# A hybrid S5 and attention trunk: the S5 stage with its first input columns in halves, chunks in pairs, two blocks in float32, and its stages in another order

## The chip, the cores and the metric

The kernel runs on one core of one Trainium2 chip. The metric is the time of one execution on the device, in microseconds (us). A core has five engines that run on their own, each in the order of its own queue: TensorE (PE, matrix products, with weight loads listed as PEld), VectorE (DVE), ScalarE (ACT), GpSimd (POOL), and SyncE (SP), which here only issues DMAs. They wait for each other at semaphores.

## The reference

Two layers on 256 tokens of width 1024, all in float32. Each layer adds half a SwiGLU of the normed stream, then a mixer, then half another SwiGLU. The first layer's mixer is an S5 state-space layer, the second's a block-sparse attention. The change concerns S5:

```python
u = h @ w_in                                     # 256 x 1024, 64 groups of 16 columns
bu = einsum(u, bb)                               # per group: 16 inputs -> 64 complex states
st = associative_scan(lam, bu)                   # st[t] = lam * st[t-1] + bu[t], complex
y = real part of einsum(st, c) + d_skip * u
g = gelu(y)
g = g * sigmoid(g @ w_glu)
h = h + g @ w_out
```

## The kernel before, in words

One program does the phases f00, s5, f01, f10, moba and f11 one after the other. `f..` are the feed-forward parts. Weights come from memory as raw float32 units of 1 MB in three buffers (class `Stream`, `RAW = 3`). A unit is loaded into a buffer as soon as the unit three places before it is freed. Each unit has two halves. `split` turns a half into a high part (`whi`, ACT, L84 or L90) and a low part (`wlo`, DVE, L85 or L91) in a format that TensorE multiplies in one pass; when the second half is split, the raw buffer is free. A product of two float32 matrices is then three products, high by high, high by low, low by high (`mm3`). `st.pump()` splits the next half ahead of its use, where the code calls it: the splits take their place in the queues of ACT and DVE at that point. The order of instructions in each queue is the order of the Python calls; nothing moves them.

S5 works through 8 blocks of 128 columns. The steps, with the lines of the profile:

- `w_in(nh, t)` (L397 to L399, tile pM): half of the columns (512) for token half t, 24 products; ACT copies the result to `us` (L976), DVE transposes it in 32x32 pieces into `U` (L977). Four calls.
- `t1(b)` (L986): block b of U times a table TA, 16 small float32 products; the result is in pA for the first four blocks and in one of the two pM buffers after that.
- `rot(b)`: on DVE two products with a table TE (L1006, L1007), a difference and a sum into `zi` (L1008, L1009), and two scans along time into `zo` (L1011); then on POOL two products (L1015, L1016) and a sum and a difference (L1017, L1018) into `hr`. The filling `rh` of the scan comes from ACT (L995), and two memsets (L994, L1005) from DVE.
- `y_out(b)` (L1044): 24 small float32 products of U and hr with a table TB into one of the two PSUM buffers pR; ACT applies Gelu into `yg`, of which there is one (L1048); DVE transposes it into `gs`, of which there are two (L1051).
- `g_tr(b)` (L1060): TensorE transposes gs into a pR buffer; ACT makes the high part of g (L1062), DVE the low part (L1063), ACT then a float32 copy `gf` (L1064).
- `glu(b)` (L1077 to L1079): block b of `g @ w_glu`, transposed, 8 column blocks of 3 products of 256 columns, accumulated over b in pA 0 to 3. `gate(i)` (L1088 to L1093): sigmoid, product with gf, high and low part.
- `so(b, t, n)` (L397 to L399, tile pA): the product with w_out.

The order around the change, `t1` and `rot` running some blocks ahead of `y_out` and `glu`:

```python
        w_in(1, 0, {3: [lambda: t1rot(0)], 5: [lambda: t1rot(1)]})
        w_in(1, 1, {1: [lambda: t1rot(2)], 4: [lambda: t1ld(3)]}, ())
        ...
        for b in range(3, NB):
            y_out(b)
            glu(b - 3)
            if b + 3 < NB:
                t1rot(b + 3)
            g_tr(b - 1)
```

A hook `{3: [...]}` is called before the fourth of the eight row blocks of a product. The tables TA, TE and TB (three buffers each) are loaded by SP (`ld_a`, `ld_e`, `ld_b`), in one queue with the weights.

Of the kernel before, what the change touches and what calls it, by code (L numbers as in the profile page):

```python
# [118 lines left out]
def trunk_kernel(ctx: ExitStack, tc, x, ffn_norm, ffn_w_gate, ffn_w_up, ffn_w_down, mix_norm,  # L119
# [3 lines left out]
    nc = tc.nc  # L123
# [28 lines left out]

    units = []
    where = {}
    GAIN = {"f00": None, "f01": 8, "f10": 16, "f11": 24, "s5": 32, "moba": 40}

    def add(key, load, gains=None):

        where[key] = len(units)
        units.append((key, load, gains))  # L160

    ahead = []

# [34 lines left out]
    def s5_units():  # L198
        for nh in range(2):
            for a in range(2):  # L200
                add(("win", nh, a), ld_cols(s5_w_in[0], a * 512, nh * 512), GAIN["s5"] + 4 * a)
        for b in range(4):
            add(("glu", b), ld_rows(s5_w_glu[0], b * 256))
        for b in range(4):
            add(("so", b), ld_rows(s5_w_out[0], b * 256))

    QKV = [("k", 0), ("q", 0), ("k", 1), ("q", 1), ("v", 0), ("v", 1)]
    QOFF = {"q": 0, "k": 1024, "v": 2048}
# [749 lines left out]
    def s5(nxt, entry):  # L958
# [12 lines left out]
        def w_in(nh, t, hooks, pumps=(1, 5)):  # L971
            uA, uB = where["win", nh, 0], where["win", nh, 1]
# [3 lines left out]
            nc.scalar.activation(us, ps, AF.Identity, scale=Rr[t])  # L976
            V.transpose(U[:, nh * 16:(nh + 1) * 16, t, :], us.rearrange("p (q c) -> p q c", c=32))  # L977

        def t1(b):
            tv = TA.pop(b).rearrange("p (i q c) -> p i q c", i=2, c=128)  # L980
# [5 lines left out]
                        mm(ps[r, c:c + 64], tv[:, i, q, r], U[:, 4 * b + q, :, :], start=True, stop=True)  # L986
            S[b] = ps

        def rot(b):
            sv = S.pop(b).rearrange("p (i q c) -> p i q c", i=2, c=64)  # L990
            e = TE.pop(b)
            ec, es = (e[:, None, i] for i in range(2))
            rh = wp.tile([128, 4, 65], F32, name="rh", bufs=2)
            V.memset(rh[:, :, 0:1], 0.0)  # L994
# [3 lines left out]
            zi = wp.tile([128, 2, 4, 65], F32, name="zi", bufs=1)  # L998
# [7 lines left out]
            V.tensor_tensor(wv[0], sv, bc(ec, 1), op=OP.mult)  # L1006
            V.tensor_tensor(wv[1], sv, bc(es, 1), op=OP.mult)  # L1007
            V.tensor_tensor(zi[:, 0, :, 1:65], wv[0][:, 0], wv[1][:, 1], op=OP.subtract)  # L1008
            V.tensor_tensor(zi[:, 1, :, 1:65], wv[0][:, 1], wv[1][:, 0], op=OP.add)  # L1009
            for i in range(2):  # L1010
                V.tensor_tensor_scan(zo[:, i].rearrange("p q c -> p (q c)"),  # L1011
                                     rh.rearrange("p q c -> p (q c)"),
                                     zi[:, i].rearrange("p q c -> p (q c)"), 0.0, op0=OP.mult, op1=OP.add)
            z = zo[:, :, :, 0:64]
            P.tensor_tensor(pv[0], z, bc(ec, 0), op=OP.mult)  # L1015
# [5 lines left out]
        def t1ld(b):  # L1021
            t1(b)
            if b + 3 < NB:
                ld_a(b + 3)

        def t1rot(b):
            t1ld(b)
            rot_ld(b)

        def rot_ld(b):  # L1030
            rot(b)
            if 0 < b < NB - 2:
                ld_e(b + 2)

        def y_out(b):
            tb = TB.pop(b)
            v2 = tb[:, 0:1024].rearrange("p (i q c) -> p i q c", i=2, c=128)
            v3 = tb[:, 1024:1536].rearrange("p (q c) -> p q c", c=128)
            ps = psR()
            hr = H.pop(b)  # L1040
            for q in range(4):
                for i, (v, z) in enumerate(((v3[:, q], U[:, 4 * b + q]), (v2[:, 0, q], hr[:, 0, q]), (v2[:, 1, q], hr[:, 1, q]))):
                    for r in HALVES:
                        mm(ps[r, q * 64:(q + 1) * 64], v[:, r], z, start=i == 0, stop=i == 2)  # L1044
# [3 lines left out]
            nc.scalar.activation(yg.rearrange("p q t c -> p (q t c)"), ps[:, 0:256], AF.Gelu_apprx_tanh)  # L1048
            gs = wp.tile([128, 2, 4, 32], F32, name="gs", bufs=2)
            for t in range(2):  # L1050
                V.transpose(gs[:, t], yg[:, :, t, :])  # L1051
            GS[b] = gs

        def g_tr(b):
            ps = psR()
            gs = GS.pop(b)
            if b == 0:
                GT["h"], GT["l"] = home(xp, "g")
            for t in range(2):
                nc.tensor.transpose(ps[:, t * 128:(t + 1) * 128], gs[:, t].rearrange("p q c -> p (q c)"),  # L1060
                                    ident)
            nc.scalar.activation(GT["h"][:, b, :], ps[:, 0:256], AF.Copy)  # L1062
            V.tensor_tensor(GT["l"][:, b, :], ps[:, 0:256], GT["h"][:, b, :].bitcast(F32), op=OP.subtract)  # L1063
            nc.scalar.activation(gf[b // 2][:, b % 2, :], ps[:, 0:256], AF.Copy)  # L1064

        def glu(b, os=range(8)):

            u = where["glu", b // 2]
            if b == 0:
                for i in range(4):  # L1070
                    acc[i] = psA(i)
            gh, gl = GT["h"][:, b, :], GT["l"][:, b, :]
            wh, wl = st.get(u, b % 2)
            for o in os:
                d = acc[o // 2][:, (o % 2) * 256:(o % 2) * 256 + 256]
                c = slice(o * 128, o * 128 + 128)
                mm(d, wh[:, c], gh, start=b == 0 and o % 2 == 0, stop=False, skip_group_check=True)  # L1077
                mm(d, wh[:, c], gl, start=False, stop=False, skip_group_check=True)
                mm(d, wl[:, c], gh, start=False, stop=b == NB - 1, skip_group_check=True)  # L1079
                if o == 7:  # L1080
                    st.release(u, b % 2)
                if o == 3 and b < 5 or o == 7 and b in (3, 4) or o == 5 and b == 4:
                    st.pump()

        def gate(i):

# [5 lines left out]
            V.tensor_copy(gh, g)  # L1092
            V.tensor_tensor(gl, g, gh.bitcast(F32), op=OP.subtract)  # L1093

        def so(b, t, n, last=False):
# [15 lines left out]
        rot_ld(4)  # L1111
        y_out(2)
        g_tr(1)
        t1rot(5)
        for b in range(3, NB):
            y_out(b)
            glu(b - 3)
            if b + 3 < NB:
# [334 lines left out]
```

## Time and profile before

| | |
|---|---|
| median of 3 runs | 991.57 us (990.74 to 991.60) |
| profiled execution | 991.97 us, of which its span 990.0 us |
| mean granted TensorE clock | 0.995 |
| PE busy | 974.4 us (98%) |
| DVE, ACT, POOL busy | 702.8 (71%), 559.7 (57%), 192.4 us (19%) |
| first product of S5, first product of so | at 214.65 and 296.52 us of the span |

Times in the profile count from the start of the span. A matrix instruction's listed length is longer than its distance to the next one, since they overlap; what one costs is read from two starts. A float32 product that isn't split is listed as two instructions. Idle time stands with the instruction that ended it, with what it waited for.

### The profile page before, as it was taken

How to read it: one execution, taken by the hardware profiler on the slowest of the kernel's cores; microseconds unless marked ns; L12 is line 12 of the kernel's file. 1: busy time of each engine (PE TensorE's matmuls, PEld its weight loads, DVE VectorE, ACT ScalarE, POOL GpSimd, SP SyncE). 2: the span in 40 equal slices, each digit the busy share in tenths (PEclk: the TensorE clock that was granted, in tenths of full speed). 3: DMA queues.
4: the chain of work that ended last, by engine and by line, in shares of the span. 5: the costliest groups of instructions: out<-in, count | busy, mean ns of one | idle time of the engine just before them, and what ended most of it. 6: DMA issues, size and time to landing. Idle time of an engine off the chain costs nothing.

```text
span 990.0 us, 17176 instructions
## 1 busy us (share of the span) xinstructions
PE 974.4 (98%) x6695; PEld 868.0 (88%) x6695; DVE 702.8 (71%) x1148; ACT 559.7 (57%) x997; POOL 192.4 (19%) x361
## 2 busy tenths in 40 slices
PE   8999999999899999999999999999999999999998
PEld 7788888887788999999999999998888899999997
DVE  5899767768978676666667766665689667766662
ACT  6556766553255665555445555554898655655540
POOL 6963444414720100000010000000441010000000
PEclk9999999999899999999999999999999999999999
DMA  8978877886556565556536655553445546756531
GB/s 236 319 246 272 274 262 239 301 318 225 216 183 199 173 213 179 205 173 211 171 127 213 224 200 185 191 182 132 133 165 170 161 139 218 249 171 213 171 128 42
DMA packets 140000, 198.71 MB, mean 201 GB/s; under 512 B 18232, under 2 KB 111504, under 8 KB 139664
## 3 DMA queue, kind: packets, MB, share of 16 engines
q1 hardware_dynamic: 133808, 184.32, 57.3%
q0 software_dynamic: 5536, 12.71, 3.6%
q8 instruction: 52, 0.85, 0.4%
q10 hardware_dynamic: 576, 0.61, 0.3%
q14 instruction: 28, 0.23, 0.1%
HBM read 183.89 MB, written 13.66 MB: 200 GB/s over the span
## 4 chain that ended last, share of the span: by engine, by line
PE 89%; DVE 5%; issue 2%; POOL 1%; DMA 1%; ACT 1%; DVEq 0%; ACTq 0%; POOLq 0%; SPq 0%
PE pM L552 12%; PE pM L551 12%; PE pM L553 12%; PE pA L397 10%; PE pA L399 10%; PE pA L398 9%; PE pM L397 6%; PE pM L398 6%; PE pM L399 6%; DVE zo L1011 1%; PE pR L331 1%; DMA raw<-in_ffn_w_up_dram 1%; DVE wlo L85 1%; PE pR L862 1%; DVE zi L1008 1%
## 5 line engine op out<-in xcount | busy, mean ns | idle before, releaser
L551 PE MATMUL pM<-xa,whi 128*128 128x256 f32 x1056 | 295.7, 280 | 0.0
L552 PE MATMUL pM<-xa,whi 128*128 128x256 f32 x1056 | 294.9, 279 | 0.0
L553 PE MATMUL pM<-xa,wlo 128*128 128x256 f32 x1056 | 294.6, 279 | 0.0
L91 DVE SCALAR_TENSOR_TENSOR wlo<-raw,gT,whi 128x512 fp32r<-128x512 f32 x328 | 228.1, 748 | 70.3 <-ACT whi L90 70.1
L85 DVE TENSOR_TENSOR wlo<-raw,whi 128x1024 fp32r<-128x1024 f32 (+1 forms) x157 | 190.7, 1229 | 55.9 <-ACT whi L84 54.9
L90 ACT ACTIVATE whi<-raw,gT 128x512 fp32r<-128x512 f32 x328 | 213.7, 711 | 19.2 <-PE pA L399 14.6
L552 PEld LDWEIGHTS pM<-xa,whi 128*128 128x128 f32 x1056 | 198.5, 188 | 2.6
L551 PEld LDWEIGHTS pM<-xa,whi 128*128 128x128 f32 x1056 | 198.5, 188 | 2.3
L553 PEld LDWEIGHTS pM<-xa,wlo 128*128 128x128 f32 x1056 | 198.5, 188 | 0.0
L84 ACT ACTIVATE whi<-raw 128x1024 fp32r<-128x1024 f32 (+1 forms) x157 | 161.3, 1050 | 25.1 <-PE pA L399 7.7
L397 PE MATMUL pA<-whi,ah 128*128 128x512 f32 x352 | 138.8, 394 | 0.0
L398 PE MATMUL pA<-wlo,ah 128*128 128x512 f32 x352 | 137.6, 391 | 0.0
L399 PE MATMUL pA<-whi,al 128*128 128x512 f32 x352 | 137.6, 391 | 0.0
L566 ACT ACTIVATE sg<-gr 128x256 f32<-128x256 f32 x66 | 27.6, 418 | 165.7 <-DVE gr L563 165.7
L397 PE MATMUL pM<-whi,xa 128*128 128x512 f32 x288 | 119.4, 415 | 0.0
L398 PE MATMUL pM<-wlo,xa 128*128 128x512 f32 x288 | 113.1, 393 | 0.1
L399 PE MATMUL pM<-whi,xa 128*128 128x512 f32 x288 | 112.7, 391 | 0.0
L346 POOL TENSOR_TENSOR ms<-ss 128x1 f32<-128x1 f32 x10 | 1.9, 193 | 472.5 <-ACT sq L343 472.5
L399 PEld LDWEIGHTS pA<-whi,al 128*128 128x128 f32 x352 | 66.1, 188 | 14.4
L397 PEld LDWEIGHTS pA<-whi,ah 128*128 128x128 f32 x352 | 66.1, 188 | 11.6
L398 PEld LDWEIGHTS pA<-wlo,ah 128*128 128x128 f32 x352 | 66.2, 188 | 11.3
L563 DVE TENSOR_TENSOR gr<-pM,rrow 128x512 f32<-128x512 f32 x66 | 45.5, 690 | 40.8 <-PE pM L553 40.7
(263 smaller groups left out, 1237.5 us busy)
## 6 DMA issues: line engine op xcount, KB each, us to landing
raw<-in_ffn_w_down_dram SPq DMA_DIRECT2D x44, 1024.0 KB, 5.5
raw<-in_ffn_w_gate_dram SPq DMA_DIRECT2D x80, 512.0 KB, 4.0
raw<-in_ffn_w_up_dram SPq DMA_DIRECT2D x80, 512.0 KB, 5.1
raw<-in_moba_w_qkv_dram SPq DMA_DIRECT2D x12, 1024.0 KB, 5.2
TB<-dB SPq DMA_DIRECT2D x8, 768.0 KB, 5.8
raw<-in_ffn_w_gate_dram SPq DMA_DIRECT2D x16, 256.0 KB, 4.4
raw<-in_ffn_w_up_dram SPq DMA_DIRECT2D x16, 256.0 KB, 4.7
dB<-tt POOLq DMA_DIRECT2D x16, 256.0 KB, 5.4
```

The lines of the kernel that those rows point to most:

```text
L84: nc.scalar.activation(hi[:, c], r[:, c], AF.Copy)
L85: nc.vector.tensor_tensor(lo[:, c], r[:, c], hi[:, c].bitcast(F32), op=OP.subtract)
L90: nc.scalar.activation(hi[:, c], r[:, c], AF.Identity, scale=g)
L91: nc.vector.scalar_tensor_tensor(lo[:, c], r[:, c], g, hi[:, c].bitcast(F32), op0=OP.mult, op1=OP.subtract)
L397: mm(o, xh, wh, start=start, stop=False)
L398: mm(o, xh, wl, start=False, stop=False)
L399: mm(o, xl, wh, start=False, stop=stop)
L551: mm(o, a, xh, start=k == 0 and i == 0, stop=False, skip_group_check=True)
L552: mm(o, a, xl, start=False, stop=False, skip_group_check=True)
L553: mm(o, b, xh, start=False, stop=k == 7, skip_group_check=True)
L563: V.tensor_tensor(gr, ps.rearrange("p (i c) -> p i c", i=2), Rr["row"][:, None, :].to_broadcast([128, 2, 256]), op=OP.mult)
L566: nc.scalar.activation(sg, gr[:, 0, :], AF.Silu)
```

## The change

- The first 512 columns of w_in are done in two halves of 256 for both token halves each; the second 512 as before.
- `t1` is called for two blocks at once (`t1x2`), with the loads of the next tables behind both; `y_out` mostly in pairs.
- For the first two blocks (`WHOLE = 2`), glu is one float32 product from the raw unit and gf instead of three: these two halves are not split, g isn't split for them, and their raw buffer is freed when glu(1) has used it.
- The filling zeros of rh and zi are set once by POOL. The two transposes of yg are one. In gate, the high part is made by ACT, not by DVE.
- The calls stand in another order, and the pumps at other places (`PUMPS`; two at once in the last w_in). The order of the weight units is the same. g's place in its buffer is offset by 124 columns, not 8.

```diff
-XO = {'f00': 124, 's5': 124, 'g': 8, 'f01': 80, 'f10': 8, 'moba': 124, 'f11': 8}
+XO = {'f00': 124, 's5': 124, 'g': 124, 'f01': 80, 'f10': 8, 'moba': 124, 'f11': 8}
...
             self.first[u] = len(self.halves)
-            self.halves += [(u, 0), (u, 1)]
+            if not units[u][3]:
+                self.halves += [(u, 0), (u, 1)]
...
+            add(key, ld_rows(w[0], key[1] * 256), whole=key[0] == "glu" and 2 * key[1] < WHOLE)
...
+        RH = [wp.tile([128, 4, 65], F32, name=f"rh{i}") for i in range(2)]
+        ZI = wp.tile([128, 2, 4, 65], F32, name="zi")
+        for a in RH:
+            P.memset(a[:, :, 0:1], 0.0)
+        P.memset(ZI[:, :, :, 0:1], 0.0)
+
+        def w_in(c0, n, t, hooks, last, pumps=(1, 5)):
+
+            us_ = [where["win", c0 // 512, a] for a in range(2)]
             ps = psM()
-            product(ps, t, uA, uB, hooks, pumps)
+            ts = slice(t * 128, t * 128 + 128)
+            for k in range(8):
+                for f in hooks.get(k, ()):
+                    f()
+                u = us_[k // 4]
+                wh, wl = st.get(u, (k % 4) // 2)
+                c = (k % 2) * 512 + c0 % 512
+                mm3(ps[:, 0:n], X["h"][:, k, ts], X["l"][:, k, ts], wh[:, c:c + n], wl[:, c:c + n], k == 0, k == 7)
+                if k % 2:
+                    if k in pumps:
+                        st.pump()
+                    if last:
+                        st.release(u, (k % 4) // 2)
...
+        def t1x2(b):
+            for a in (b, b + 1):
+                t1(a)
+            for a in (b, b + 1):
+                if a + 3 < NB:
+                    ld_a(a + 3)
...
-            V.memset(zi[:, :, :, 0:1], 0.0)
...
-            for t in range(2):
-                V.transpose(gs[:, t], yg[:, :, t, :])
+            V.transpose(gs, yg.rearrange("p q t c -> p t q c"))
...
-            nc.scalar.activation(GT["h"][:, b, :], ps[:, 0:256], AF.Copy)
-            V.tensor_tensor(GT["l"][:, b, :], ps[:, 0:256], GT["h"][:, b, :].bitcast(F32), op=OP.subtract)
+            if b >= WHOLE:
+                nc.scalar.activation(GT["h"][:, b, :], ps[:, 0:256], AF.Copy)
+                V.tensor_tensor(GT["l"][:, b, :], ps[:, 0:256], GT["h"][:, b, :].bitcast(F32), op=OP.subtract)
             nc.scalar.activation(gf[b // 2][:, b % 2, :], ps[:, 0:256], AF.Copy)
...
+                if b < WHOLE:
+                    mm(d, w[:, c], g, start=first, stop=last, skip_group_check=True)
+                else:
+                    mm(d, wh[:, c], gh, start=first, stop=False, skip_group_check=True)
+                    mm(d, wh[:, c], gl, start=False, stop=False, skip_group_check=True)
+                    mm(d, wl[:, c], gh, start=False, stop=last, skip_group_check=True)
+                for _ in range(PUMPS.get((b, o), 0)):
+                    st.pump()
+                if o == 7 and b >= WHOLE:
                     st.release(u, b % 2)
-                if o == 3 and b < 5 or o == 7 and b in (3, 4) or o == 5 and b == 4:
-                    st.pump()
+                elif o == 7 and b % 2:
+                    st.free_raw(u)
...
-            V.tensor_copy(gh, g)
+            nc.scalar.activation(gh, g, AF.Copy)
...
-        w_in(0, 0, entry_hooks("s5") if entry else {})
-        w_in(0, 1, {})
-        w_in(1, 0, {3: [lambda: t1rot(0)], 5: [lambda: t1rot(1)]})
-        w_in(1, 1, {1: [lambda: t1rot(2)], 4: [lambda: t1ld(3)]}, ())
-        rot_ld(3)
-        y_out(0)
-        y_out(1)
-        t1ld(4)
-        g_tr(0)
-        rot_ld(4)
+        PUMPS = {(0, 1): 1, (0, 3): 1, (3, 1): 1, (3, 5): 1, (4, 1): 1, (4, 5): 1, (5, 1): 1, (5, 5): 1}
+        w_in(0, 256, 0, entry_hooks("s5") if entry else {}, False)
+        w_in(0, 256, 1, {}, False, ())
+        w_in(256, 256, 0, {7: [lambda: t1x2(0), lambda: rot(0)]}, False, (1, 3))
+        w_in(256, 256, 1, {}, True, ())
+        w_in(512, 512, 0, {0: [lambda: rot(1)], 2: [lambda: t1x2(2)], 4: [lambda: rot(2), lambda: warm(AF.Gelu_apprx_tanh)]}, False, ())
+        w_in(512, 512, 1, {1: [lambda: rot(3)], 3: [lambda: y_out(0), lambda: y_out(1)], 5: [lambda: st.pump(2)],
+                           7: [lambda: g_tr(0)]}, True, ())
+        GT["h"], GT["l"] = home(xp, "g")
+        g_tr(1)
+        glu(0, range(4))
+        t1x2(4)
+        rot(4)
+        glu(0, range(4, 8))
         y_out(2)
-        g_tr(1)
-        t1rot(5)
-        for b in range(3, NB):
-            y_out(b)
-            glu(b - 3)
-            if b + 3 < NB:
-                t1rot(b + 3)
-            g_tr(b - 1)
+        y_out(3)
+        rot(5)
+        glu(1)
+        g_tr(2)
+        t1x2(6)
+        rot(6)
+        g_tr(3)
+        glu(2)
+        y_out(4)
+        y_out(5)
+        rot(7)
+        glu(3)
+        g_tr(4)
+        g_tr(5)
+        y_out(6)
+        y_out(7)
+        glu(4)
+        g_tr(6)
         wstack.close()
         lstack.close()
         XP[0] = xstack.enter_context(tc.tile_pool(name="xt2", bufs=1))
         g_tr(7)
-        st.pump(2)
+        glu(5)
         warm(AF.Sigmoid)
-        glu(5)
         for i in range(4):
             glu(6, (2 * i, 2 * i + 1))
             glu(7, (2 * i, 2 * i + 1))
```

More of the change, by code (lines that the diff above doesn't have):

```diff
@@ L154, in trunk_kernel, with add @@
     where = {}
+    WHOLE = 2
     GAIN = {"f00": None, "f01": 8, "f10": 16, "f11": 24, "s5": 32, "moba": 40}
-    def add(key, load, gains=None):
+    def add(key, load, gains=None, whole=False):
         where[key] = len(units)
-        units.append((key, load, gains))
+        units.append((key, load, gains, whole))
     ahead = []
@@ L201, in s5_units @@
                 add(("win", nh, a), ld_cols(s5_w_in[0], a * 512, nh * 512), GAIN["s5"] + 4 * a)
[L202 to L205, printed above, removed]
+        for key in (('glu', 0), ('glu', 1), ('glu', 2), ('glu', 3), ('so', 0), ('so', 1), ('so', 2), ('so', 3)):
+            w = s5_w_glu if key[0] == "glu" else s5_w_out
+            add(key, ld_rows(w[0], key[1] * 256), whole=key[0] == "glu" and 2 * key[1] < WHOLE)
     QKV = [("k", 0), ("q", 0), ("k", 1), ("q", 1), ("v", 0), ("v", 1)]
@@ L969, in s5 @@
               .rearrange("p (f c) -> p f c", c=256) for i in range(4)]
-        def w_in(nh, t, hooks, pumps=(1, 5)):
-            uA, uB = where["win", nh, 0], where["win", nh, 1]
-            ps = psM()
-            product(ps, t, uA, uB, hooks, pumps)
+        RH = [wp.tile([128, 4, 65], F32, name=f"rh{i}") for i in range(2)]
[5 more added lines that the diff above has]
+            us_ = [where["win", c0 // 512, a] for a in range(2)]
+            ps = psM()
+            ts = slice(t * 128, t * 128 + 128)
[11 more added lines that the diff above has]
+                        st.release(u, (k % 4) // 2)
             us = wp.tile([128, 512], F32, name="us", bufs=1)
-            nc.scalar.activation(us, ps, AF.Identity, scale=Rr[t])
-            V.transpose(U[:, nh * 16:(nh + 1) * 16, t, :], us.rearrange("p (q c) -> p q c", c=32))
+            nc.scalar.activation(us[:, 0:n], ps[:, 0:n], AF.Identity, scale=Rr[t])
+            V.transpose(U[:, c0 // 32:(c0 + n) // 32, t, :], us[:, 0:n].rearrange("p (q c) -> p q c", c=32))
         def t1(b):
@@ L992, in rot @@
             ec, es = (e[:, None, i] for i in range(2))
-            rh = wp.tile([128, 4, 65], F32, name="rh", bufs=2)
-            V.memset(rh[:, :, 0:1], 0.0)
+            rh, zi = RH[b % 2], ZI
             nc.scalar.activation(rh[:, :, 1:65], rho[:, 4 * b:4 * b + 4, None].to_broadcast([128, 4, 64]), AF.Copy)
@@ L1019, in rot @@
             H[b] = hr
-        def t1ld(b):
-            t1(b)
-            if b + 3 < NB:
[L1024 to L1031, printed above, removed]
             if 0 < b < NB - 2:
@@ L1056, in g_tr @@
             gs = GS.pop(b)
-            if b == 0:
-                GT["h"], GT["l"] = home(xp, "g")
             for t in range(2):
@@ L1068, in glu @@
             u = where["glu", b // 2]
[L1069 to L1073, printed above, removed]
+            g = gf[b // 2][:, b % 2, :]
+            if b < WHOLE:
+                w = st.raw[u][:, b % 2 * 1024:b % 2 * 1024 + 1024]
+            else:
+                gh, gl = GT["h"][:, b, :], GT["l"][:, b, :]
+                wh, wl = st.get(u, b % 2)
             for o in os:
+                first, last = b == 0 and o % 2 == 0, b == NB - 1
+                if first:
+                    acc[o // 2] = psA(o // 2)
                 d = acc[o // 2][:, (o % 2) * 256:(o % 2) * 256 + 256]
                 c = slice(o * 128, o * 128 + 128)
[L1077 to L1080, printed above, removed]
+                if b < WHOLE:
+                    mm(d, w[:, c], g, start=first, stop=last, skip_group_check=True)
+                else:
+                    mm(d, wh[:, c], gh, start=first, stop=False, skip_group_check=True)
[4 more added lines that the diff above has]
+                if o == 7 and b >= WHOLE:
                     st.release(u, b % 2)
-                if o == 3 and b < 5 or o == 7 and b in (3, 4) or o == 5 and b == 4:
-                    st.pump()
+                elif o == 7 and b % 2:
+                    st.free_raw(u)
         def gate(i):
```

2 lines of the change are left out of this document (removed).

## The prediction

> **What bounds the kernel now.** I read the page first, in its line of engines.
>
> ```profile
> PE 974.4 (98%) x6695; PEld 868.0 (88%) x6695; DVE 702.8 (71%) x1148; ACT 559.7 (57%) x997; POOL 192.4 (19%) x361
> ```
>
> TensorE (PE) is busy for 98% of the span, so over the whole kernel only fewer or faster products could help. But the change is confined to the S5 mixer, and an average says nothing of a stage. So next come stretches of S5: length, then busy time of PE, PEld, DVE, ACT and POOL, the granted clock, the DMA share and GB/s.
>
> ```profile
> 228.24:246.50 18.26, 18.26 (x296) 14.97 (x295) 17.95 (x32) 4.95 (x9) 10.93 (x10) 1.00 0.60 212
> 246.50:251.00 4.50, 0.52 (x4) 0.37 (x2) 4.11 (x7) 0.24 (x1) 3.14 (x4) 0.79 0.65 207
> ```
>
> From 228 us on VectorE (DVE) is the full engine: 17.95 of 18.26 us, then 4.11 of 4.50 us in which PE does 0.52. TensorE stands still in S5 for want of DVE. PE's instructions in order of time give the sizes (start, length, and in brackets the idle time before and what ended it); below them the row of the waits that stands behind two of the three (total, count, longest).
>
> ```profile
> 214.65 0.48 PE L397 MATMUL pM<-whi,xa 128*128 128x512 f32 x1
> 216.12 0.60 PE L331 MATMUL pR<-cst,h 128*128 128x128 f32 x4
> 216.48 0.48 PE L397 MATMUL pM<-whi,xa 128*128 128x512 f32 x1
> 227.69 0.39 PE L398 MATMUL pM<-wlo,xa 128*128 128x512 f32 x1
> 227.92 0.39 PE L399 MATMUL pM<-whi,xa 128*128 128x512 f32 x1
> 228.24 1.15 PE L986 MATMUL pA<-U,TA 128*64 128x64 f32 x32
> 229.32 0.50 PE L397 MATMUL pM<-whi,xa 128*128 128x512 f32 x1
> 242.36 0.34 PE L1044 MATMUL pR<-U,TB 128*64 128x64 f32 x4
> 245.38 1.15 PE L986 MATMUL pM<-U,TA 128*64 128x64 f32 x32
> 250.51 0.69 PE L1060 MATMUL pR<-cst,gs 128*128 128x128 f32 x2 [3.98 <-DVE gs L1051]
> 258.10 0.28 PE L1077 MATMUL pA<-xa,whi 128*128 128x256 f32 x1
> 258.45 0.28 PE L1077 MATMUL pA<-xa,whi 128*128 128x256 f32 x1
> 269.25 0.44 PE L1060 MATMUL pR<-cst,gs 128*128 128x128 f32 x2 [1.46 <-ACT gf L1064]
> 276.20 0.56 PE L1060 MATMUL pR<-cst,gs 128*128 128x128 f32 x2 [1.94 <-ACT gf L1064]
> 287.29 0.60 PE L1060 MATMUL pR<-cst,gs 128*128 128x128 f32 x4
> 296.52 0.47 PE L397 MATMUL pA<-whi,xa 128*128 128x512 f32 x1 [0.22 <-DVE xa L1092]
> ```
>
> ```profile
> ACT gf L1064 <- DVE xa L1063: 17.8, 8, 6.2
> ```
>
> Three stalls, 3.98 + 1.46 + 1.94 = 7.4 us, all before a g_tr (L1060) and all DVE's in the end: it delivers gs late, or its copy of g (L1063) holds back ACT's gf. The clock adds to that (half-us stretches; the third number from the right is the clock):
>
> ```profile
> 249.00:249.50 0.50, 0.00 (x0) 0.00 (x0) 0.50 (x1) 0.00 (x0) 0.10 (x1) 0.57 0.81 237
> 255.50:256.00 0.50, 0.50 (x16) 0.50 (x16) 0.50 (x2) 0.00 (x0) 0.00 (x0) 0.60 1.34 450
> 276.00:276.50 0.50, 0.30 (x2) 0.20 (x2) 0.05 (x1) 0.50 (x3) 0.50 (x1) 0.88 1.07 442
> 279.50:280.00 0.50, 0.50 (x5) 0.50 (x4) 0.00 (x0) 0.48 (x2) 0.50 (x2) 0.71 0.00 0
> ```
>
> PE runs at half clock from 249.1 to 255.9 and from 276.4 to 279.8. It works for 5.4 and 3.4 us of these and loses half: 2.7 + 1.7 = 4.4 us. So stalls and clock cost about 12 us in S5, and that is all the change can win. All times below are from the profiled execution (991.97 us); the median of the runs is 991.57, and I carry the difference over to it. About 0.2% (2 us) is what a measurement of this kernel can tell from no change.
>
> **The prices.** From the PE rows: a 512-column product takes 0.23 us (227.69 to 227.92); three split 256-column products 0.35 (258.10 to 258.45), so 0.117 each; the four transposes of a prep 0.4 (216.12 to 216.48); one t1 1.08 (228.24 to 229.32); two y_out 3.0 (242.36 to 245.38); a glu block 8 x 0.35 + 0.1 = 2.9; two g_tr 0.7, taken as prep's four with their handovers; from g_tr(6) to the first product of so 9.2 (287.29 to 296.52). A whole float32 product of 256 columns stands in the attention stage:
>
> ```profile
> 729.75 0.60 PE L1214 MATMUL pA<-kT,qT 128*128 128x256 f32 x2
> 730.00 0.58 PE L397 MATMUL pM<-whi,xa 128*128 128x512 f32 x1
> 730.42 0.40 PE L398 MATMUL pM<-wlo,xa 128*128 128x512 f32 x1
> ```
>
> From 729.75 to 730.42 is 0.67, less 0.23 for the product of L397 between: 0.44 for one product, which the profile lists as two. The other engines:
>
> ```profile
> 229.44 0.69 DVE L1006 TENSOR_TENSOR wv<-pA,TE 128x512 f32<-128x512 f32 x1 [0.15 <-PE pA L986]
> 232.68 0.06 DVE L994 MEMSET rh<- 128x4 f32 x1
> 238.23 1.19 DVE L85 TENSOR_TENSOR wlo<-raw,whi 128x1024 fp32r<-128x1024 f32 x1
> 239.34 0.70 DVE L977 STREAM_TRANSPOSE U<-us 128x512 f32<-128x512 f32 x1
> 240.00 0.67 DVE L1006 TENSOR_TENSOR wv<-pA,TE 128x512 f32<-128x512 f32 x1
> 242.90 1.81 DVE L1011 TENSOR_TENSOR_SCAN zo<-rh,zi 128x260 f32<-128x260 f32 x2
> 250.17 0.47 DVE L1051 STREAM_TRANSPOSE gs<-yg 128x128 f32<-128x128 f32 x2
> 251.65 0.42 DVE L1063 TENSOR_TENSOR xa<-pR,xa 128x256 fp32r<-128x256 f32 x1
> 261.95 2.18 DVE L85 TENSOR_TENSOR wlo<-raw,whi 128x1024 fp32r<-128x1024 f32 x1
> ```
>
> ```profile
> 261.76 1.28 POOL L1015 TENSOR_TENSOR pv<-zo,TE 128x512 f32<-128x512 f32 x1 [1.29 <-issue]
> ```
>
> ```profile
> 250.76 0.38 ACT L1048 ACTIVATE yg<-pR 128x256 f32<-128x256 f32 x1 [5.61 <-DVE gs L1051]
> 258.10 1.05 ACT L84 ACTIVATE whi<-raw 128x1024 fp32r<-128x1024 f32 x1
> ```
>
> A rotation alone costs DVE 3.3 us (229.44 to 232.7); beside POOL's half of the one before it 5.5 (232.7 to 238.2) or 4.7 (240.00 to 244.71). A split (L85) takes 1.2 alone and 2.2 beside POOL: it waits for the POOL instruction under way (261.76 + 1.28 = 263.04) and runs after it. And a Gelu on ACT waits until DVE has read the one yg buffer.
>
> **The change on the PE path.** The first columns in halves: 96 x 0.117 = 11.2 us for 48 x 0.23 = 11.0, so +0.2. Sixteen float32 products for sixteen threes: 16 x (0.44 - 0.35) = +1.4. They take two splits (2 x 1.2) and two L1063 copies (2 x 0.4) from DVE, 3.2 us, and about as much from ACT. The memsets that leave DVE are 0.06 each; the three that POOL gets stand ahead of the second row factor, which is needed at about 221 (below): nothing. One transpose of 128x256 in place of two lies between 0.24, half the pair, and 0.70, L977's with twice the elements; I take the pair's 0.47. The cast in gate goes from DVE to ACT, beside glu products: -0.2 (the stall before 296.52) to +0.2; I take nothing. The new offset of g: w_in reads at the new one and glu at the old one, at the same price per column; nothing, 0.3 either way.
>
> **The order, walked through.** *Start.* From 214.65: prep 0.4, two quarters of 2.8 (220.9), 7/8 of the third, t1(0) at 223.4, not 228.24. Rot(0) runs to about 228; the U transposes behind it wait for the fourth quarter, to 229.7. Rot(1), (2), (3), beside POOL, get 4.3 (POOL begins earlier in it), 5.1 and 5.0, with a U transpose between: end at 244.8. PE does two t1 pairs, the rest of w_in and y_out(0), (1), and comes to g_tr(0) at 244.5.
>
> *Early waits.* gs(0) is ready at 245.3: 0.8 us. ACT's second Gelu waits for it too, and behind that in ACT's queue stand two splits (1.9) and then gf(0): ready at 247.9, and glu(0), free at 246.7, waits 1.2. DVE does these splits, each behind a POOL instruction, until 250.2; the last U transpose stands behind both, to 250.9, and t1(4), free at 249.7, waits 1.3. Together 3.3 us.
>
> *Middle.* Four t1 (4.3), twelve float32 products (5.3), glu(2), two y pairs and two g_tr with handovers: from 251.0 to 269.9 PE waits for nothing, and DVE (rot 4 to 6) stays ahead.
>
> *Late wait.* gs(5) ends at 270.7, rot(7) at 273.9; then come the two splits that glu(3) pumped, the second behind POOL, to 277.4; only then the copy of g(4) (0.4) and ACT's gf(4) (0.4), which frees the PSUM buffer of y_out(6): 278.2. PE is through with glu(3) and two g_tr at 273.5 and stands 4.7 us. Without that buffer it would still stand, at y_out(7), for POOL's half of rot(7).
>
> *End.* 3.0 for the y pair, 2.9 for glu(4), 9.2 to so: 293.3. The late stall brings the half clock, 1.7 or 2.7 as in the two cases above; 2.2 makes it 295.5. After that the order is as before.
>
> So reaching so at 295.5, not 296.52, gives -1.0 us. By terms: stalls 8.0 for 7.4, clock 2.2 for 4.4, products +1.6: 0.0, and I leave the 1.0 between the two ways as their error. I go by the walk. With rotations known to 0.4 us each it is good to some 2 us.
>
> [...]
>
> **Rivals.** *Clock stays up:* without a half clock after the late stall 2.2 us more are won: -3.2, 988.4. Against it stands the stall of 1.94 that brought one. *Rotations run free:* if rot(1) to (3) cost DVE about 4.0, between 3.3 alone and the 4.7 to 5.5 seen, rot(3) ends 2.4 us sooner, the early waits shrink to under 1, and PE hands that on to the end: -1.0 - 2.4 = -3.4, 988.2; at 3.3 it is 987. *Slower, a clock that falls early:* the waits of 1.2 and 1.3 us stand within 4.4 us of each other; if the clock halves there too it costs 1.7 to 2.7, and with the longer case at the late stall the sum is -1.0 + 2.7 + 0.5 = +2.2, 993.8. [...] *Slower, a late weight block:* glu(0)'s raw buffer is now held until glu(1) ends, at 261.4, and only then can the load of glu(6)'s block start; ACT comes to its split at 270.6, with gf(4) queued behind.
>
> ```profile
> DMA to landing us min/median/max: 2.8/5.0/14.0
> ```
>
> Raw blocks in S5 land after 5.0 us in the median, 14.0 at most. Over 9.2 the stall of y_out(6) grows by the excess, up to 4.8: +3.8, 995.4.
>
> **Numbers.** Forecast 0.48; clock stays up 0.08; rotations free 0.19; early clock 0.15; late block 0.10. The forecast's own range is 989 to 993. The whole range, 987.0 to 994.0, takes in the rivals but for the worst of the late block. Faster by over 0.2%: 0.08 + 0.19 and 0.06 of the forecast's lower end, 0.33. Slower: 0.15 + 0.10 less the part under 2 us, 0.22. Within: 0.45.
>
> **What would show it.** In the profile after: t1(0) near 223.4 us; PE's waits of 0.8, 1.2 and 1.3 us before g_tr(0), glu(0) and t1(4); one of 4 to 5 us before y_out(6), behind DVE's copy and ACT's gf; half clock once, after it; so at 295 to 296 us; the stages after S5 unchanged. I am wrong if the late wait is under 2 us, if PE waits in the middle part, or if later stages shift by other than S5's gain.

## The result, and the profile after

The changed kernel takes 990.06 us, the kernel before 991.57 (medians of 22 runs each, 988.64 to 991.52 and 990.74 to 992.49). The ratio is 0.9985, with a 95% interval of 0.9978 to 0.9991: 1.5 us faster, 0.9 to 2.2. The profiled execution took 989.0 us, of which its span is 987.0. The page's line of engines hardly moved, and says again nothing of S5:

```profile
PE 971.7 (98%) x6727; PEld 868.0 (88%) x6727; DVE 695.9 (71%) x1118; ACT 560.3 (57%) x1000; POOL 192.8 (20%) x364
```

PE's instructions of the changed kernel in order of time, the stages that the prediction walked through, and a row of the stage behind S5:

```profile
214.08 0.36 PE L398 MATMUL pM<-whi,xa 128*128 128x256 f32 x1
222.95 2.08 PE L1005 MATMUL pA<-U,TA 128*64 128x64 f32 x64
244.79 0.44 PE L1068 MATMUL pR<-cst,gs 128*128 128x128 f32 x2 [0.61 <-DVE gs L1061]
247.43 1.99 PE L1091 MATMUL pA<-gf,raw 128*128 128x256 f32 x8 [1.25 <-ACT gf L1073]
250.49 2.08 PE L1005 MATMUL pM<-U,TA 128*64 128x64 f32 x64 [1.07 <-DVE U L996]
257.38 3.72 PE L1091 MATMUL pA<-gf,raw 128*128 128x256 f32 x16
260.94 0.38 PE L1068 MATMUL pR<-cst,gs 128*128 128x128 f32 x2
278.03 0.48 PE L1055 MATMUL pR<-U,TB 128*64 128x64 f32 x4 [4.76 <-ACT gf L1073]
294.25 0.40 PE L398 MATMUL pA<-whi,xa 128*128 128x512 f32 x1
...
326.42 0.61 PE L364 MATMUL pR<-rdiag,ones 128*128 128x128 f32 x4
```

The last of these rows stood here in the kernel before:

```profile
329.50 0.61 PE L363 MATMUL pR<-rdiag,ones 128*128 128x128 f32 x4
```

Of the three stalls of before, the one at g_tr(0) is down from 3.98 to 0.61, and the other two (1.46 and 1.94) are gone; three others have come, 1.25 and 1.07 early and 4.76 late. The sum is 7.7 for 7.4. From 251 to 273 us PE waits for nothing. The row behind S5 is 3.08 us earlier. Of that 0.57 was there before S5 began (214.08 for 214.65); S5 up to the first product of so takes 80.17 for 81.87, 1.70 less; and from there to that row it is 32.17 for 32.98, 0.81 less. Behind that row nothing has changed: to the end of the span it is 660.6 for 660.5.

Behind the late stall, VectorE (DVE) and ScalarE (ACT):

```profile
272.62 1.28 DVE L1034 TENSOR_TENSOR_SCAN zo<-rh,zi 128x260 f32<-128x260 f32 x2
273.82 3.41 DVE L86 TENSOR_TENSOR wlo<-raw,whi 128x1024 fp32r<-128x1024 f32 x2
277.15 0.41 DVE L1072 TENSOR_TENSOR xa<-pR,xa 128x256 fp32r<-128x256 f32 x1
...
277.59 0.38 ACT L1073 ACTIVATE gf<-pR 128x256 f32<-128x256 f32 x1 [4.12 <-DVE xa L1072]
```

The chain is the forecast one: rot(7)'s scans, the two splits, the copy of g(4), gf(4), y_out(6). In stretches (length, busy time of PE, PEld, DVE, ACT, POOL, granted clock, DMA share, GB/s), the stall and what follows, and below them the middle part:

```profile
274.47:277.88 3.41, 0.00 (x0) 0.00 (x0) 3.09 (x3) 0.29 (x2) 3.41 (x2) 1.00 0.01 2
277.88:281.29 3.41, 3.26 (x61) 3.26 (x62) 0.42 (x1) 1.08 (x4) 1.89 (x3) 0.50 0.89 262
...
252.00:270.00 18.00, 17.87 (x330) 16.21 (x327) 14.22 (x24) 3.44 (x10) 10.61 (x10) 1.00 0.83 304
```

The clock halves once, as the stall ends, and PE works 3.26 us at half: 1.6 lost. And in the middle part, where PE is full, DVE is idle for 3.8 of 18.0 us, just before it becomes the engine that everything waits for. Whether work that DVE does late could have been done there is what the experiments ask.

### The profile page after: what moved, and what is told of

The parts are those of the page before. It is cut to its first block, busy times and chain, and to the rows that moved or that the text cites. A ratio compares the mean times of both kernels' runs of the same rounds, so it can differ in the third digit from the quotient of the medians.

```text
span 987.0 us, 17215 instructions
## 1 busy us (share of the span) xinstructions
PE 971.7 (98%) x6727; PEld 868.0 (88%) x6727; DVE 695.9 (71%) x1118; ACT 560.3 (57%) x1000; POOL 192.8 (20%) x364
## 4 chain that ended last, share of the span: by engine, by line
PE 92%; DVE 4%; DMA 1%; POOL 1%; issue 1%; ACT 1%; SPq 0%; ACTq 0%
PE pM L553 13%; PE pM L552 13%; PE pM L554 12%; PE pA L398 10%; PE pA L400 10%; PE pA L399 10%; PE pM L398 6%; PE pM L399 6%; PE pM L400 6%; PE pR L1055 1%; PE pR L332 1%; DVE wlo L86 1%; PE pR L863 1%; DVE zo L1034 1%; PE pA L1091 1%
## 5 line engine op out<-in xcount | busy, mean ns | idle before, releaser
L85 ACT ACTIVATE whi<-raw 128x1024 fp32r<-128x1024 f32 (+1 forms) x155 | 159.2, 1050 | 24.9 <-PE pA L400 7.9
L398 PE MATMUL pM<-whi,xa 128*128 128x512 f32 (+1 forms) x304 | 122.1, 402 | 0.0
L399 PE MATMUL pM<-wlo,xa 128*128 128x512 f32 (+1 forms) x304 | 115.8, 381 | 0.1
L400 PE MATMUL pM<-whi,xa 128*128 128x512 f32 (+1 forms) x304 | 115.5, 380 | 0.0
```

The source lines that it names most:

```text
L85: nc.scalar.activation(hi[:, c], r[:, c], AF.Copy)
L398: mm(o, xh, wh, start=start, stop=False)
L399: mm(o, xh, wl, start=False, stop=False)
L400: mm(o, xl, wh, start=False, stop=stop)
```

## The experiments

Each is an edit of the changed kernel unless it says otherwise. Times are medians, and ratios are to the kernel before, measured beside them.

### The late splits

```diff
-PUMPS = {(0, 1): 1, (0, 3): 1, (3, 1): 1, (3, 5): 1, (4, 1): 1, (4, 5): 1, ...
+PUMPS = {(0, 1): 1, (0, 3): 1, (4, 0): 1, (4, 1): 1, (4, 2): 1, (4, 5): 1, ...
```

> The changed kernel, with the two splits that glu(3) calls moved into glu(4); nothing else. Theory (VectorE's queue order makes the late stall: the copy of g(4) stands behind two splits that nobody needs before glu(6)): rot(7) ends at 273.9 us, the copy and gf follow at once, y_out(6) starts at about 274.7 (stall 1.4 in place of 4.8), y_out(7) then waits some 1.6 for POOL's half of rot(7), which no longer shares with the splits, and there is no half clock: 3.0 us less than the changed kernel's 990.06, 987.0. Rival (POOL's half of rot(7) is the bound whatever the splits do, ending at 279.8): y_out(7) starts at 279.8, glu(4) at 281.3 in place of 282.45, 1.1 us less: 989.0. Second rival (the two splits only move the stall to glu(6) or so, since VectorE is full): no gain, 990.

988.75 us (987.67 to 989.12), ratio 0.997 [0.9959, 0.9981]: 1.3 us gained where 3.0 were expected. PE's waits from the late stall on, in order of time, then DVE's and ACT's rows behind the last:

```profile
275.04 0.34 PE L1055 MATMUL pR<-U,TB 128*64 128x64 f32 x4 [1.41 <-ACT gf L1073]
277.76 0.34 PE L1055 MATMUL pR<-hr,TB 128*64 128x64 f32 x4 [0.99 <-POOL hr L1040]
278.44 0.34 PE L1055 MATMUL pR<-hr,TB 128*64 128x64 f32 x4 [0.35 <-POOL hr L1041]
293.11 0.50 PE L398 MATMUL pA<-whi,xa 128*128 128x512 f32 x1 [0.63 <-ACT xa L1110]
...
281.24 4.63 DVE L86 TENSOR_TENSOR wlo<-raw,whi 128x1024 fp32r<-128x1024 f32 x4 [0.50 <-ACT whi L85]
...
286.24 0.38 ACT L1073 ACTIVATE gf<-pR 128x256 f32<-128x256 f32 x1 [1.92 <-DVE xa L1072]
291.09 0.58 ACT L1106 ACTIVATE sg<-pA 128x512 f32<-128x512 f32 x1
```

The place of the splits does make the stall: 1.41 and 1.34 remain of it, as expected, and the clock stays up (1.00 in every stretch from 274.47 to 287.47). But the four splits are now in one block, gf(6) stands behind them on ACT, behind it two more splits and the load of the table for the sigmoid (1.28 us from 289.69), and so waits for gate. So the second rival had its share: a part of what is taken from DVE's queue at one place comes back at the next.

### The early splits

```diff
-w_in(512, 512, 1, {..., 5: [lambda: st.pump(2)], 7: [lambda: g_tr(0)]}, True, ())
+w_in(512, 512, 1, {..., 7: [lambda: g_tr(0)]}, True, ())
-PUMPS = {(0, 1): 1, (0, 3): 1, ...
+PUMPS = {(0, 1): 1, (0, 3): 1, (0, 5): 1, (0, 7): 1, ...
```

> The changed kernel, with the two splits that stand in the last w_in moved behind rot(4), into the second half of glu(0); nothing else. Theory (from 224 to 262 us VectorE is the bound, so a wait taken from TensorE there comes back where the next rotation is due): the waits of 1.2 and 1.1 us before glu(0) and t1(4) go, but waits of about 0.9 and 1.7 appear before glu(2) and y_out(5), y_out(6) starts where it did, 990.0 +- 0.5. Rival (the two waits stand in TensorE's own chain and are handed on to the end): 2.3 us less, 987.8.

990.37 us (989.26 to 992.38), 0.9988 [0.9979, 0.9997], no gain. From the view of the waits (total, count, longest):

```profile
PE pR L1055 <- ACT gf L1073: 6.2, 2, 4.8
PE pA L1094 <- DVE xa L1072: 0.7, 1, 0.7
```

The waits before glu(0) and t1(4) are gone; one of 0.7 stands before glu(2), one of 1.47 before y_out(5), and the late one is unchanged at 4.8. The theory holds: in that part DVE sets the pace, and PE's waits are only where it shows.

### The clock behind the late stall

```diff
         g_tr(5)
+        pd = psM()
+        wd = st.get(where["glu", 2], 0)[0]
+        for j in range(38):    # 19 in the second run
+            mm(pd[:, 0:256], wd[:, 0:128], GT["h"][:, 2, :], start=True, stop=True)
         y_out(6)
```

> The changed kernel with 38 extra products of 256 columns (0.117 us each, 4.4 us together, results not used) in TensorE's queue between g_tr(5) and y_out(6), where it stands still for 4.76 us. Theory (the still stand brings the half clock, and that costs): no half clock after it, y_out(6) at 278.0 as before, y_out(7) at 279.85, when POOL's half of rot(7) is there, glu(4) at 281.3 in place of 282.45: 1.1 us less, 989.0, and the runs scatter less than 988.6 to 991.5. Rival (the clock falls for another reason, or costs nothing): 990, with the half clock at the same place.

> The changed kernel with 19 extra products (2.2 us, results not used) in the late stall in place of 38: 2.5 us of standing still are left. Theory (one stretch of about 1.9 us, as in the kernel before, is enough for the half clock): half clock after it as in the changed kernel, 990 +- 0.5. Rival (the clock falls only for a longer stretch, and the one of 1.9 us had help from the waits before it): no half clock, 988 as with the whole stall filled.

Filled, 987.80 us (987.24 to 989.54), 0.9966 [0.9953, 0.9979]; half filled, 987.87 (987.76 to 989.56), 0.9966 again. Useless products save 2.2 us in the median, where 1.1 were expected. Between the profiled executions it is 1.2, by the way from the start of S5 to so: 78.97 for 80.17. The clock stays up (y_out(6) of the filled kernel, and the stretch that was at half clock in the unfilled one):

```profile
278.05 0.34 PE L1055 MATMUL pR<-U,TB 128*64 128x64 f32 x4 [0.33 <-ACT gf L1073]
...
277.88:281.29 3.41, 3.22 (x97) 3.02 (x97) 0.87 (x2) 1.16 (x4) 1.91 (x3) 1.00 0.83 274
```

The half fill's profile says more. It leaves one late wait, with no half clock after it:

```profile
277.99 0.34 PE L1055 MATMUL pR<-U,TB 128*64 128x64 f32 x4 [2.54 <-ACT gf L1073]
```

So the rival was right that a length alone does not decide: 1.94 us brought the half clock in the kernel before, 2.54 didn't here. Its reason, help from the waits before the 1.94, isn't shown (the section on the hardware). Nor does the same stall do the same in every execution. The mean clock that is recorded for each is 1.0 in three of the five half-filled ones (987.76 to 987.87 us), as in the profiled one, but 0.997 and 0.998 in the two that took 989.10 and 989.56: there a half clock did come. In the five filled ones it is 0.999 or 1.0.

> The changed kernel itself once more, for a second profiled execution. Theory (its scatter of 988.6 to 991.5 is the half clock behind the late stall, which costs more or less by where in the stall it begins; with the stall filled the runs lay at 987.2 to 988.1 but for one): the median is near 990.06 again, and in a profile whose time lies above 989.5 the half clock covers more of TensorE's work than the first profile's 3.3 us, the rows before 273 us being the same. Rival (the scatter is from before S5 or from the tables' loads): the half clock is as before, and the difference stands at the start of S5 or at t1(3).

The same kernel again: 989.80 us (988.89 to 991.74), 0.998 [0.997, 0.9989]. Its profiled execution took 989.53, and had one stretch at half clock of the same length:

```profile
214.53 0.36 PE L398 MATMUL pM<-whi,xa 128*128 128x256 f32 x1
232.24 1.15 PE L1005 MATMUL pA<-U,TA 128*64 128x64 f32 x32 [0.92 <-DMA TA<-dA]
...
279.05:282.46 3.41, 3.41 (x70) 3.41 (x68) 0.55 (x2) 0.77 (x2) 1.24 (x2) 0.51 0.71 286
```

The 0.5 us between the two profiles is in the start of S5, 214.53 for 214.08, as the rival had it. These two profiles don't show what makes the scatter up to 991.5, but the mean clocks of the first 22 executions show a part of it. Ten have 0.997 or 0.998, like the two profiled ones (0.998 and 0.997), with a median of 989.4 us; twelve have 0.996 or less, with a median of 990.7. A mean of 0.996 takes at least 6.9 us at half clock (an estimate: up to 0.9965 before rounding, so twice 0.0035 of the span of 987.0 us). One stretch of 3.41 us, as in each of these profiles, doesn't make that. So in more than half of the executions the clock was down for longer than in either profile; where in the kernel isn't recorded. This fits with filling having saved more in the median (2.2) than between the profiles (1.2). In the run with whole columns below, a late stall of the same 4.76 us brought two stretches at half clock, with 1.12 + 3.41 us of work in them. The clock isn't all of the scatter: the filled run of 989.54 has a mean clock of 1.0.

### The parts, in the changed order

```diff
-    WHOLE = 2
+    WHOLE = 0
...
-w_in(512, 512, 1, {..., 5: [st.pump(2)], 7: [g_tr(0)]}, True, ())
+w_in(512, 512, 1, {..., 5: [st.pump(2)]}, True, ())
+g_tr(0)
```

> The changed kernel, with all blocks split and in three products, none in float32 (WHOLE = 0); g_tr(0) moves behind the last w_in, where g's buffer is free. Theory (the float32 products cost TensorE 1.4 us and relieve VectorE, the bound, of two splits and two copies, 3.2 us alone and up to 5 beside POOL): without them glu(0) waits 4 us or more for splits of its own, and the time rises by 4 to 5 us, 994.5. Rival (VectorE's part is hidden, and only TensorE's products count): 1.4 us less, 988.7.

995.53 us (994.52 to 998.92), 1.0048 [1.0034, 1.0061]: 5.5 us slower than the changed kernel. Two waits stand in glu(0), for DVE's part of g and ACT's:

```profile
PE pA L1094 <- DVE xa L1072: 2.4, 1, 2.4
PE pA L1093 <- ACT xa L1071: 1.8, 1, 1.8
```

A part of the 5.5 us is the clock: in its profile it is at half for 3.41 us behind these waits and for 6.83 behind the late stall, 10.2 in all for 3.4 in the changed kernel.

```diff
-w_in(0, 256, 0, ...); w_in(0, 256, 1, ...)
-w_in(256, 256, 0, {7: [t1x2(0), rot(0)]}, ...); w_in(256, 256, 1, ...)
-w_in(512, 512, 0, {0: [rot(1)], ...
+w_in(0, 512, 0, ...); w_in(0, 512, 1, ..., True, (1, 3))
+w_in(512, 512, 0, {0: [t1x2(0), rot(0), rot(1)], ...
```

> The changed kernel with its first 512 input columns whole again (two calls of w_in in place of four), t1(0), t1(1), rot(0) and rot(1) at the start of the next call; all else as changed. Theory (VectorE bounds S5 from the first rotation to the eighth, so the time at which the first one starts is handed on): t1(0) starts at about 227 us in place of 223, waiting for the U transpose, and g_tr(0), y_out(6) and the end come 3 to 4 us later: 993.5. Rival (the early rotations run into the wait for tables, POOL and U anyway, so the halves bring little): within 1 us of 990.06.

994.26 us (992.80 to 994.73), 1.0027 [1.0016, 1.0039]: 4.2 slower. PE's rows, then the two stretches behind its late stall:

```profile
227.39 2.09 PE L1005 MATMUL pA<-U,TA 128*64 128x64 f32 x64 [1.62 <-issue]
248.51 0.44 PE L1068 MATMUL pR<-cst,gs 128*128 128x128 f32 x2 [2.00 <-DVE gs L1061]
282.94 0.48 PE L1055 MATMUL pR<-U,TB 128*64 128x64 f32 x4 [4.76 <-ACT gf L1073]
...
280.65:284.06 3.41, 1.12 (x20) 1.12 (x22) 2.24 (x3) 1.04 (x3) 3.33 (x4) 0.51 0.23 29
284.06:287.47 3.41, 3.41 (x69) 3.41 (x68) 0.45 (x1) 0.38 (x1) 0.69 (x2) 0.50 0.70 283
```

The first rotation starts 4.4 us later, y_out(6) 4.9 later. Here too a part is the clock, which is at half four times as long as in the changed kernel (13.65 us, half of it behind the wait before g_tr(0)). In this order the two parts are worth 5.5 and 4.2 us.

### The float32 products alone, in the old order

The kernel before, with `WHOLE = 2`, its branches in g_tr and glu, and the two halves left out of the queue of splits as the only edit. The pumps stand where they stood, so each splits a later half.

> The kernel before with the float32 products of the first two blocks as the only change (no splits and no copies for them), in the old order. Theory (what VectorE is spared counts only where VectorE is what TensorE waits for, and in the old order the spared splits lie behind the early stall of 4.0 us): stalls later in S5 shrink by about 1.4, which the slower products eat: 991.6, within 0.7 of before. Rival (the spared 3.2 us of VectorE are worth as much here as they were in the changed order, where taking them back cost 5.5 us): 988 or less.

991.04 us (990.39 to 991.60), 0.9996 [0.9986, 1.0006]: nothing that can be told from before. PE's waits before a g_tr:

```profile
249.56 0.52 PE L1062 MATMUL pR<-cst,gs 128*128 128x128 f32 x2 [3.98 <-DVE gs L1053]
268.14 0.44 PE L1062 MATMUL pR<-cst,gs 128*128 128x128 f32 x2 [0.56 <-ACT gf L1067]
275.10 0.44 PE L1062 MATMUL pR<-cst,gs 128*128 128x128 f32 x2 [1.98 <-ACT gf L1067]
```

The 3.98 before the first g_tr is untouched, the next falls from 1.46 to 0.56, the third stays. The same part that is worth 5.5 us in the changed order is worth 0.5 here (991.57 less 991.04), which the interval doesn't tell from nothing, and no more than 1.4.

### Another order

All parts kept; the rotations go as early as their inputs allow, glu fills in behind them, and the splits stand where DVE has room:

```diff
+PUMPS = {}
+w_in(512, 512, 1, {1: [rot(3)], 3: [y_out(0), y_out(1)], 7: [g_tr(0)]}, True, ())
+g_tr(1) moved behind y_out(3); then, P for one st.pump():
+P, glu(0, 0..3), t1x2(4), rot(4), P, y_out(2), rot(5), glu(0, 4..7), P, y_out(3),
+g_tr(1), t1x2(6), g_tr(2), y_out(4), glu(1), rot(6), P, glu(2, 0..3), g_tr(3), y_out(5),
+glu(2, 4..7), g_tr(4), rot(7), glu(3, 0..3), P, glu(3, 4..7), y_out(6), g_tr(5),
+glu(4, 0..3), g_tr(6), P, P, glu(4, 4..7), glu(5, 0..3), y_out(7), P, glu(5, 4..7),
+g_tr(7), P, P
```

> The changed kernel with another order and other places for the splits, all its other parts kept. No split in the last w_in; the rotations 4 to 7 and the y_out follow as early as their inputs allow, glu and its halves fill in behind them; the splits of blocks 6 and 7 and of so stand behind y_out(6) and after, where VectorE has time. In order: split, glu(0) first half, t1 4 and 5, rot 4, split, y 2, rot 5, glu(0) second half, split, y 3, g_tr 1, t1 6 and 7, g_tr 2, y 4, glu(1), rot 6, split, glu(2) first half, g_tr 3, y 5, glu(2) second half, g_tr 4, rot 7, glu(3) with a split between its halves, y 6, g_tr 5, glu(4) with g_tr 6 and two splits between its halves, glu(5) with y 7 and a split between its halves, g_tr 7, two splits. Theory (the stalls of both kernels are the place of splits and copies in VectorE's queue, not its amount of work): no stall above 1.5 us, no half clock, 6 to 7 us less than the changed kernel: 983.5. Rival (VectorE and POOL together have too much work, and the stalls come back elsewhere): 987 or more.

982.85 us (982.47 to 983.05), 0.9914 [0.9899, 0.9929]: 8.6 us faster than before, and 7.2 faster than the changed kernel by the order and the places of the splits alone. All of PE's waits in S5, and the middle part:

```profile
PE pA L398 <- ACT xa L1110: 0.6, 1, 0.6
PE pR L1068 <- DVE gs L1061: 0.6, 1, 0.6
PE pA L1094 <- DVE xa L1072: 0.4, 1, 0.4
```

```profile
252.00:270.00 18.00, 18.00 (x284) 16.41 (x283) 16.25 (x26) 6.80 (x15) 14.46 (x12) 1.00 0.86 301
```

DVE now does 16.25 us of its work in the part where PE is full, in place of 14.22, and no wait of over 0.6 us is left; the clock stays up. The moves were made together, so what each of them brought isn't known beyond the two runs on the splits above.

Then each part is taken out of this order, by the same edits as above (without the float32 products, two more splits stand ahead of glu(0)):

> The new order with all blocks split and in three products (WHOLE = 0, two more splits ahead of glu(0), g_tr(0) behind the last w_in). Theory (VectorE is the bound up to 262 us in any order, so the two splits and two copies come back in full as waits of TensorE before glu(0) and y_out(4), with a half clock): 8 us more than the new order's 982.85, 991. Rival (in the new order VectorE has room, and only the products count): 1.4 us less, 981.5.

> The new order with the first input columns whole again, t1(0), t1(1), rot(0) and rot(1) at the start of the next call. Theory (the start of the first rotation is handed on, as it was in the changed order, where it cost 4.2 us): t1(0) at 227.4, waits before g_tr(0), 4 to 5 us more than 982.85: 987.5. Rival (the new order has slack for it): within 1 us of 982.85.

Without the float32 products it takes 993.14 us (991.88 to 996.32), 1.0021 [1.0011, 1.003], 10.3 more; with whole columns 986.91 (986.23 to 988.67), 0.9953 [0.9936, 0.9969], 4.1 more. The main waits of the first, then of the second:

```profile
PE pR L1055 <- ACT gf L1073: 3.7, 1, 3.7
PE pA L1093 <- ACT whi L85: 3.0, 1, 3.0
```

```profile
PE pR L1068 <- DVE gs L1061: 2.1, 1, 2.1
PE pA L1005 <- issue: 1.6, 1, 1.6
```

So the order needs both parts. In this order the float32 products save 10 us, though the products themselves are slower, and in the old one nothing that can be told. Only this one place of the two extra splits was tried; another might cost less.

The smaller parts of the change (the zeros by POOL, the single transpose, the cast in gate, g's offset, the calls in pairs) were not taken out one by one. One more came with it: the load of ACT's table for Gelu (1.28 us) stands at 229.55 us, in the kernel before at 243.47, just ahead of the first Gelu. It was not what g_tr(0) waited for there, since DVE was in rot(3) until 250.2.

## Why the prediction was right, step by step

Forecast were 990.6 us, 1.0 less than before, by stalls of 8.0 for 7.4, a half clock of 2.2 for 4.4, and products of +1.6. Measured were 990.06, 1.5 less. The mechanism held in the profile, wait by wait; that the median came so close is in part luck, as the points on the clock and on the sizes show.

- *Start and prices.* t1(0) was walked to 223.4 and started at 222.95; from the first product of S5 that is 8.75 and 8.87. (Two sums of the walk are off by 0.2 to 0.3: 214.65 + 0.4 + two quarters of 2.8 is 220.65, not 220.9, and the terms of the middle part make 19.2, not 18.9.) Sixteen float32 products: the eight of glu(1) take 260.94 - 257.38 = 3.56, 0.445 each, for 0.44. Three rotations beside POOL were walked to 244.8; the scans of the last ended at 244.4:

```profile
242.59 1.81 DVE L1034 TENSOR_TENSOR_SCAN zo<-rh,zi 128x260 f32<-128x260 f32 x2
```

  *Rotations run free* was wrong.
- *Stalls.* 0.8, 1.2, 1.3 and 4.7 were walked; 0.61, 1.25, 1.07 and 4.76 were measured, each with the releaser named. The middle part has no wait. *A late weight block* did not come: the load of glu(6)'s block was issued at 259.2 and landed 7.7 us later, at 266.9; ACT came to its split at 270.45.
- *Clock.* Once, behind the late stall, as forecast. Its price of 2.2 was 1.6 in the profile and 2.2 by the medians of the filled kernels, which is more than one stretch. *Clock stays up* and *a clock that falls early* were wrong for the profiled execution. For the median the latter isn't excluded: twelve of the 22 executions had more half clock than the profile shows, where isn't known. And what the clock gained on the 4.4 of before (2.2 forecast, 2.8 measured) was gained between these two profiles, whose mean clocks are 0.995 and 0.998. Over all executions the means are 0.9960 before (53 executions beside the experiments) and 0.9966 after (22); times the span that is 3.9 and 3.4 us lost at most, an estimate of 0.5 us gained.
- *Mis-sized.* The walk ends with so at 295.5, the trace at 294.25. Of the difference of 1.25, 0.57 lies before S5, and 0.6 is the clock. And "after that the order is as before" left out 0.81 (a later stage that shifts by other than S5's gain was one of the prediction's own signs of being wrong): in the kernel before, so began while DVE was still at the low part of its first block (L1093, to 297.10); its first products started 0.3 apart (the first at 296.52, the third at 297.16, the fourth at 297.49; a product takes 0.23), while in the changed kernel they are 0.23 apart from the first on. That is 0.3 of the 0.81; the rest is in gaps too small to name. The products, too, were mis-sized: S5 without its waits and without what the half clock took is 81.87 - 7.38 - 0.22 - 4.40 = 69.87 us before and 80.17 - 7.69 - 1.63 = 70.85 after, +1.0 for the forecast +1.6. Which part of the S5 path got the 0.6 back isn't shown.
- *What stayed unsaid.* The prediction held the stalls and the clock to be "all the change can win", about 12 us, and had them return as others. It didn't say that they need not: the late stall is made by two splits that nobody wants before glu(6), while DVE had idled 3.8 us in the part before. The new order shows it: 1.6 us of waits, and no half clock before the last product.
- *Not settled.* The profiles are 3.0 us apart, the medians 1.5. The profile before lies 0.4 above its median, that after 1.1 below; between the two profiles of the changed kernel 0.45 came from the start of S5. The clock accounts for a part, as said; what makes the rest of the scatter isn't known. By the mean clocks the medians hold less of the clock than the profiles do, so the terms of the profiles don't add up to the 1.5 of the medians.

## What to carry to other kernels

Where an engine that is not the full one delivers late, look for the stage in which it idles and ask what in its queue could have been done there; moving ready work was worth 7.2 us here. A stall that is filled or removed at one place must be followed to the next queue (ACT's, here) before its price is counted. And a part of a change need not have a price by itself: the float32 products were worth 0.5, 5.5 and 10.3 us in the three orders, while the halves were worth the same, 4.2 and 4.1, in both orders in which they were tried.

## What the runs showed of the hardware

*The half clock lasted 3.41 us or 6.83, and a stall's length alone doesn't tell whether it comes.* It lasted 3.41 us in both profiles of the changed kernel (from 277.88 and from 279.05), 6.83 and 3.41 in the kernel before (to 255.9 and 279.8), 3.41 and 6.83 without the float32 products, 6.83 twice with whole columns. Its places in the kernel before, in tenths of a microsecond (the clock is the third number from the right, and its mean gives the place of the drop: 249.07, 276.38, 989.76):

```profile
249.00:249.10 0.10, 0.00 (x0) 0.00 (x0) 0.10 (x1) 0.00 (x0) 0.10 (x1) 0.85 0.94 156
276.30:276.40 0.10, 0.10 (x2) 0.10 (x2) 0.00 (x0) 0.10 (x2) 0.10 (x1) 0.89 1.09 451
989.70:989.80 0.10, 0.00 (x0) 0.00 (x0) 0.00 (x0) 0.00 (x0) 0.00 (x0) 0.82 0.00 0
```

The first lies within the stall of 3.98 us, which ended at 250.51, the second 0.18 us behind the one of 1.94, the third behind PE's last product. The stall of 1.46, which ended at 269.25, brought none. The same stretch in the kernel before, with the float32 products alone and with the half fill:

```profile
276.20:279.61 3.41, 3.41 (x51) 3.00 (x51) 2.59 (x4) 1.53 (x4) 3.33 (x3) 0.53 0.16 62
```

```profile
276.20:279.61 3.41, 3.41 (x53) 3.34 (x49) 2.58 (x4) 1.53 (x5) 3.07 (x3) 1.00 0.07 25
```

```profile
276.20:279.61 3.41, 1.62 (x54) 1.62 (x56) 1.74 (x3) 1.04 (x3) 3.33 (x3) 1.00 0.32 79
```

In the first the stall of 1.94 us ends where the stretch begins. In the second one of 1.98 had ended at 275.10, and in the third one of 2.54 ends at 277.99; in both the clock is 1.00 in every stretch from 274.47 to 287.47. Stalls of 4.76 us brought 3.41 us at half clock in the changed kernel, and 6.83 without the float32 products and with whole columns.

So a stall of 1.94 us brought the half clock, and ones of 1.98 and 2.54 did not; what decides it the runs don't show. Nor is its place the same in every execution (in the two profiles of the changed kernel the drop lies 63.8 and 64.5 us behind the start of S5), and with the half fill the mean clock is 1.0 in three executions and 0.997 and 0.998 in two: the price of one and the same stall can differ too.

*A table load became a wait.* In the changed kernel the load of t1(3)'s table is issued behind both t1(0) and t1(1), and in the second profile above PE waits 0.92 us for it. There it cost nothing: the wait before g_tr(0), 0.61 in the first profile, is gone in the second, and from the start of S5 to so it takes 80.25 us for 80.17.
